# Delta rule: where the exponentials of the decays stand, and the yield inside the inverse

## The chip, the core and the metric

One core of one Trainium2 chip runs the whole program in one launch. The metric is the device time of that launch in microseconds (us). Of the kernel before there are three timed runs, and beside them one profiled execution, from which all rows below come.

## The reference

The reference is one layer for 4096 tokens of width 1024 in fp32. A modulated input `h` is projected by `w_in`. Half of the heads do gated linear attention (GLA), the other half the gated delta rule. Both results are gated with silu, projected back by `w_out`, and go through a residual and a layer norm. The part that matters here is the delta rule, with 4 heads of 128 and chunks of 64 tokens:

```
qkv = silu(causal_depthwise_conv(h @ w_qkv))      # q, k, v per head; q and k are l2-normed
d = cumsum(g)                                      # per chunk
L = exp(where(causal, d[:, None] - d[None, :], -inf))
A = where(strict, (beta * k) @ k.T * L, 0)
u, w = triangular_solve(A + eye, [beta * v, beta * k * exp(d)])
qk = where(causal, q @ k.T * L, 0)
for each chunk:                                    # scan over the chunks
    v_new = u - w @ S
    o = (q * exp(d)) @ S + qk @ v_new
    S = exp(d[-1]) * S + (k * exp(d[-1] - d)).T @ v_new
```

`L` is the matrix of decays. Its exponentials are the ones that the change moves.

## The kernel before, in words

The program has three stages one after the other: GLA (the span's start to about 730 us), the delta rule (730 to about 1860 us), and the output projection with the layer norm (to the end).

The delta-rule stage goes through 16 blocks: 2 pairs of heads, for each 8 blocks of 512 tokens. Iteration `it` of its loop overlaps three blocks: `new` is projected and prepared, `last` (the block before) is inverted and scanned, and `done` (two before) is normed. Each iteration has two halves. In each half `weave(side, main)` runs two generators against each other: `main` is a stream of projection matmuls (tile `pp`, 128x512, three per step and eight steps per projection), `side` is the small work. A `yield n` in `side` lets `main` go `n` steps on. Each matmul of `side` is bound behind the last `main` matmul emitted before it (`side_after`); once `main` has run out, that bound falls away.

In the first half `main` is `qk_products(new)`, 32 steps: four projections, each with a convolution (ACT `u` and `cacc`, then DVE `cacc`) and a Silu on ACT into `KQ`. `side` is `first_half`: `norm_gate(done)`, `new_values(last)`, a wait until two of the four projections are there, `decay_tiles(new)`, `inverse_head(last)`, `key_side(new)`, `inverse(last)`. In the second half `main` is `vg_products(new)`, and `side` is `second_half`: `gram(new)` and four steps of `scan(last)`.

- `decay_tiles` loads the tile `E` (128 x 8 x 128) by a DMA from `d_spill`, masks it on POOL (`affine_select`, L751), and makes eight Exp on ACT (rows `E<-E,dneg` at L104), with a load of the exp table ahead of them (L109).
- `key_side` transposes the keys (`pw<-ident,KQ`), squares them on ACT (eight rows `jk`, sums in `ssk`), and makes `kdec` on DVE.
- `inverse` forms the inverse of the lower-triangular block in three groups of small matmuls with a copy on ACT between them: group 1 is `pw<-Td,AQ` (32x32), copied to `Pa` (two ACT copies, L112); group 2 is `pw<-Rd,Pa` and `pw<-Pa,Rd` (32x32), copied to `TP` and `Rt`; then `pw<-TP,AQ` and `pw<-Rt,TP` (64x64), each with a copy. `Td` is a DVE transpose.
- `gram` (second half) multiplies `KQ` by itself (`pw<-KQ`, 128x256), and DVE makes `AQ` of it with `E` as a factor. It is the only reader of `E`.
- `scan` makes `pw<-S,KQ`, `zr` on DVE, `pw<-zr,Rt`, a copy `z` on ACT, `pw<-z,kdec`, and `S` on DVE. At its first step ACT still has rows `jk` (sums in `ssq`) of the queries.

The order of the instructions on each engine is not the order in which they are written: a scheduler with its own costs sets it. Two things bind it here: `side_after`, above, and `in_order`, by which all Exp, Ln and Silu and the table loads at L109 keep their written order. The load of the Silu table has no line of its own in the program. It appears at L104 ahead of the first Silu behind an Exp.

Matmuls of fp32 appear as two rows each in the trace, so the counts of small matmuls there are twice those of the program (rows that follow one another are merged, and some records can be missing).

Of the kernel before, what the change touches and what calls it, by code (L numbers as in the profile page):

```python
# [15 lines left out]
AF = mybir.ActivationFunctionType  # L16
# [14 lines left out]
def tile_hybrid(ctx, tc, xp, x, c, wada, bada, w_gla, w_vl, w_gdn, w_out, wup, bgate,  # L31
# [33 lines left out]
    def work_psum():  # L65
        return banks["work"].tile([P, TB], F32, name="pw", tag="pw")
# [15 lines left out]
    def in_order(ins):  # L82


        if last_table[0] is not None:
            keep_after(ins, last_table[0], "table order")
        last_table[0] = ins
# [9 lines left out]
    def mm(out, lhsT, rhs, start, stop):  # L97
        pe(nc.tensor.matmul(out, lhsT=lhsT, rhs=rhs, start=start, stop=stop))  # L98
# [4 lines left out]
    def act(out, in_, func, **kw):  # L103
        ins = nc.scalar.activation(out=out, in_=in_, func=func, **kw)  # L104
        if func in (AF.Exp, AF.Ln, AF.Silu):
            in_order(ins)

    def load_table():
        in_order(nc.scalar.preload_act_table_set("natural_log_exp_and_others"))  # L109

    def copy_a(out, in_):
        nc.scalar.copy(out=out, in_=in_)  # L112
# [158 lines left out]
    def gtile(name, dt=F32):  # L271
        return const.tile([P, 2, NC2], dt, name=name)

    beta, dmid, dneg, ed, edl, een = (gtile(n) for n in ("beta", "dmid", "dneg", "ed", "edl", "een"))
# [60 lines left out]
    with ExitStack() as ph:  # L335
# [300 lines left out]
        for it in range(2 * NB + 1):  # L636
            t, b = divmod(it, NB)
            new = it < 2 * NB
# [74 lines left out]
    with ExitStack() as ph:  # L713
# [29 lines left out]
        def decay_tiles(t, b, E):  # L743

            c0 = 8 * b
            nc.sync.dma_start(out=E.rearrange("p n c -> p (n c)"), in_=dsp[t, b:b + 1].to_broadcast([P, 8 * P]))
            load_table()
            for cc in range(2):
                ns = slice(4 * cc, 4 * cc + 4)
                Ec = E[:, ns, :]  # L750
                nc.gpsimd.affine_select(out=Ec, in_=Ec, compare_op=ALU.is_ge, fill=-1e30, base=0,  # L751
                                        pattern=[[0, 4], [1, P]], channel_multiplier=-1)
                for n in range(4 * cc, 4 * cc + 4):
                    act(E[:, n], E[:, n], AF.Exp, bias=dneg[:, t, c0 + n:c0 + n + 1])

        def sumsq(KQ, which, name):

# [14 lines left out]
        def key_side(st):  # L772

            t, c0, KQ = st["t"], 8 * st["b"], st["KQ"]
            ssk, kps = sumsq(KQ, 0, "ssk")
            f_ = dp2.tile([P, 8], F32, name="f_", tag="f_")
            nc.vector.reciprocal(out=f_, in_=ssk)
            tt(f_, f_, beta[:, t, c0:c0 + 8], mul)
            fe = dp2.tile([P, 8], F32, name="fe", tag="fe")
            tt(fe, f_, een[:, t, c0:c0 + 8], mul)  # L780
            kdec = dp2.tile([P, 8, P], F32, name="kdec", tag="kdec")
            for cc in range(2):
                tt(kdec[:, 4 * cc:4 * cc + 4, :], kps[cc].rearrange("p (n c) -> p n c", c=P),
                   fe[:, 4 * cc:4 * cc + 4].unsqueeze(2).to_broadcast([P, 4, P]), mul)
            yield 2

            s = power(dp2, ssk, half, "s")
            st.update(f_=f_, kdec=kdec, s=s)
# [46 lines left out]
        def inverse_head(st):  # L835

            Rd = st["Rd"]
            Td = dp.tile([P, 8, 32], F32, name="Td", tag="Td")
            nc.vector.transpose(out=Td.rearrange("p n i -> p (n i)"), in_=Rd.rearrange("p n i -> p (n i)"))
            for bl in range(4):  # L840
                bs = slice(32 * bl, 32 * bl + 32)
                nc.gpsimd.tensor_copy(out=Rt[bs, :, bs], in_=Rd[bs])
            for bl in range(2):
                bs = slice(32 * bl, 32 * bl + 32)
                copy_a(T64[bs, :, bs], Td[bs])
            st["Td"] = Td

        def inverse(st):

            AQ, Rd, Td = st["AQ"], st["Rd"], st["Td"]  # L850

            Pa = dp.tile([P, 8, 32], F32, name="Pa", tag="Pa")

            def bank():
                return work_psum().rearrange("p (n c) -> p n c", n=8)[:, :, 0:32]
            q = [slice(32 * i, 32 * i + 32) for i in range(4)]
            pp = [bank() for _ in range(2)]
            for j in range(8):
                for i in range(2):
                    top, bot = q[2 * i], q[2 * i + 1]  # L860
                    mm(pp[i][bot, j], lhsT=AQ[top, j, 0, bot], rhs=Td[top, j], start=True, stop=True)
            for i in range(2):
                copy_a(Pa[q[2 * i + 1]], pp[i][q[2 * i + 1]])
            yield 2
            pr, pt = [bank() for _ in range(2)], bank()
            for j in range(8):
                for i in range(2):
                    top, bot = q[2 * i], q[2 * i + 1]
                    mm(pr[i][top, j], lhsT=Pa[bot, j], rhs=Rd[bot, j], start=True, stop=True)
                mm(pt[q[1], j], lhsT=Rd[q[1], j], rhs=Pa[q[1], j], start=True, stop=True)  # L870
            act(T64[q[1], :, q[0]], pt[q[1]], AF.Copy, scale=-1.0)
            for i in range(2):
                act(Rt[q[2 * i], :, q[2 * i + 1]], pr[i][q[2 * i]], AF.Copy, scale=-1.0)
            yield 2

            pp = work_psum().rearrange("p (n c) -> p n c", n=8)
            for j in range(8):
                mm(pp[64:128, j], lhsT=AQ[0:64, j, 0, 64:128], rhs=T64[:, j], start=True, stop=True)
            copy_a(Pb[64:128], pp[64:128])
            yield 2  # L880
            pr = work_psum().rearrange("p (n c) -> p n c", n=8)
            for j in range(8):
                mm(pr[0:64, j], lhsT=Pb[64:128, j], rhs=Rt[64:128, j, 64:128], start=True, stop=True)
            act(Rt[0:64, :, 64:128], pr[0:64], AF.Copy, scale=-1.0)

        def new_values(st):
            vT, s = st["vT"], st["s"]
            vp = st["vp"] = dp.tile([P, 8, P], F32, name="vp", tag="vp")
            for cc in range(2):
                pv = work_psum()  # L890
                for j in range(4):
                    ch = 2 * cc + j // 2
                    transpose(pv[:, j * P:(j + 1) * P], in_=vT[j % 2][:, ch * P:(ch + 1) * P], identity=ident)
                tt(vp[:, 4 * cc:4 * cc + 4, :], pv.rearrange("p (n c) -> p n c", c=P),
                   s[:, 4 * cc:4 * cc + 4].unsqueeze(2).to_broadcast([P, 4, P]), mul)
                yield 1
# [43 lines left out]
        def norm_gate(st):  # L940

            o, ss, sg = st["vp"], st["ss"], st["sg"]
            stt(ss, ss, 1.0 / P, st["eq"], mul, add)
            r_ = power(dp2, ss, minus_half, "r_")
            tt(o, o, r_.unsqueeze(2).to_broadcast([P, 8, P]), mul)
            yield 10
            for hh in range(2):
                po = work_psum()
                for ch in range(4):
                    transpose(po[:, ch * P:(ch + 1) * P], in_=o[:, 2 * ch + hh], identity=ident)  # L950
                yield 1
                stt(sg[:, hh], po, dnw, sg[:, hh], mul, mul)
            nc.sync.dma_start(out=ysp[st["b"], 2 + st["t"]], in_=sg)
# [35 lines left out]
        def first_half(new, last, done):  # L989
            if done is not None:  # L990
                yield from norm_gate(done)
            if last is not None:
                yield from new_values(last)
            if new is not None:
                while new.get("there", 0) < 2:
                    yield 1
                decay_tiles(new["t"], new["b"], new["E"])
                if last is not None:
                    inverse_head(last)
                yield 8  # L1000
                yield from key_side(new)
            elif last is not None:
                inverse_head(last)
                yield 3
            if last is not None:

                yield 4 if done is not None else 10
                yield from inverse(last)

        def second_half(new, last):  # L1010
            if last is not None:
# [10 lines left out]
        for it in range(2 * NB + 2):  # L1022
            t, b = divmod(it, NB)
            new, last, done = None, sts.get(it - 1), sts.pop(it - 2, None)
            if it < 2 * NB:
                new = sts[it] = dict(t=t, b=b)
# [128 lines left out]
```

## Time and profile before

| | |
|---|---|
| runs (us) | 2149.45, 2152.29, 2164.0; median 2152.29 |
| profiled execution (us) | 2148.5, of it span 2146.8 |
| mean granted TensorE clock in the span | 0.988 |
| busy in the span | PE 2064.2, DVE 1320.7, ACT 956.6, POOL 228.1 |
| PE waits, 730 to 1860 us, for ACT `Pa` | 11.5 in 15 waits |

Busy shares are averages over three stages. PE is the matmul engine; PEld, the loading of its weights, runs beside it. A wait that a row shows in brackets is idle time of that engine ahead of the row, with what ended it. PEclk is the granted TensorE clock as a share of full speed: 1.00 is 2.4 GHz, 0.50 is 1.2 GHz.

### The profile page before, as it was taken

The numbers are of one execution on the slowest core, as the hardware profiler recorded it, in microseconds if no ns is written. First come the engines' busy times: TensorE is split into PE (matmuls) and PEld (weight loads), VectorE is DVE, ScalarE is ACT, GpSimd is POOL, SyncE is SP. The second block draws the span as 40 slices with busy tenths as digits, with TensorE's granted clock in tenths as the row PEclk, the third lists the DMA queues.
The fourth block names the chain that finished last, engine by engine and source line by source line (L and its number), as shares of the span: only waits on it lengthen the run. The fifth ranks groups of instructions, "written<-read, shape, count | busy, mean of one in ns | idle before, by whom it ended". The sixth has DMA issues, their size and how long they took to land.

```text
span 2146.8 us, 34571 instructions
## 1 busy us (share of the span) xinstructions
PE 2064.2 (96%) x12809; PEld 1743.0 (81%) x12809; DVE 1320.7 (62%) x3181; ACT 956.6 (45%) x2563; POOL 228.1 (11%) x430
## 2 busy tenths in 40 slices
PE   6899999999999999999999999999999999999998
PEld 5788888888888778887888878888888888788886
DVE  7785666445335676655666666665566666676665
ACT  2655555544454544554535665445544463121110
POOL 1000000000000221111210212101221110000000
PEclk9999999999999999998999999999999999999999
DMA  8575336423423544331332443333123354353321
GB/s 316 193 254 203 141 134 227 157 102 107 168 92 118 203 172 163 95 96 46 114 116 92 139 151 104 116 103 95 56 94 116 124 182 140 140 210 143 136 103 76
DMA packets 118585, 297.17 MB, mean 138 GB/s; under 512 B 45920, under 2 KB 48144, under 8 KB 117392
## 3 DMA queue, kind: packets, MB, share of 16 engines
q1 hardware_dynamic: 118416, 294.95, 40.1%
q8 instruction: 101, 1.65, 0.3%
q14 instruction: 68, 0.56, 0.1%
HBM read 213.84 MB, written 81.07 MB: 137 GB/s over the span
## 4 chain that ended last, share of the span: by engine, by line
PE 64%; DVE 11%; ACT 9%; DMA 8%; issue 3%; POOL 2%; SPq 2%; POOLq 0%; DVEq 0%; ACTq 0%
PE pp L98 48%; PE pw L98 15%; DMA lr_raw<-lr_spill 2%; ACT jk L104 2%; PE pw L101 2%; DMA xt<-xp 2%; ACT E L104 2%; DMA r_spill<-R 1%; DVE tp L69 1%; DVE R L69 1%; ACT L104 1%; DVE vp L69 1%; DMA Rd<-r_spill 1%; DVE cacc L72 1%; DVE W L69 1%
## 5 line engine op out<-in xcount | busy, mean ns | idle before, releaser
L98 PE MATMUL pp<-h,w 128*128 128x512 f32 x4512 | 1158.9, 402 | 1.2 <-DVE W L69 1.2
L98 PEld LDWEIGHTS pp<-h,w 128*128 128x128 f32 x4512 | 824.1, 189 | 157.8 <-issue 2.0
L98 PE MATMUL pp<-w,h 128*128 128x512 f32 (+1 forms) x2112 | 421.5, 355 | 11.8 <-ACT sg L104 10.6
L98 PEld LDWEIGHTS pp<-w,h 128*128 128x128 f32 x2112 | 349.1, 189 | 65.7 <-ACT sg L104 12.0
L72 DVE SCALAR_TENSOR_TENSOR cacc<-u,convw_sb,cacc 128x512 f32<-128x512 f32 x288 | 217.4, 756 | 127.0 <-ACT cacc L104 122.2
L98 PE MATMUL pp<-wvl,h 128*128 128x280 f32 x744 | 119.9, 310 | 34.9 <-ACT h L112 26.3
L98 PEld LDWEIGHTS pp<-wvl,h 128*128 128x128 f32 x744 | 105.6, 198 | 38.7 <-ACT h L112 29.4
L69 DVE TENSOR_TENSOR tp<-U,R 128x60 f32<-128x60 f32 (+24 forms) x496 | 104.3, 210 | 14.7 <-DMA U<-u_spill 3.0
L69 DVE TENSOR_TENSOR R<-R,tp 128x60 f32<-128x60 f32 (+24 forms) x496 | 104.2, 210 | 12.8
L498 DVE COPY VS<-pw 64x256 f32<-64x256 f32 x64 | 26.7, 417 | 135.5 <-PE pw L98 135.1
L112 ACT COPY u<-pp 128x512 f32<-128x512 f32 x96 | 55.9, 582 | 119.8 <-PE pp L98 109.9
L104 ACT ACTIVATE rl<-mv,lnepscol 128x1 f32<-128x1 f32 x32 | 9.4, 294 | 217.9 <-DVE mv L703 215.8
L261 POOL TENSOR_TENSOR rs<-ss,minus_half 128x8 f32<-128x8 f32 x16 | 31.4, 1962 | 606.7 <-DVE ss L514 606.7
L98 PE MATMUL pw<-S,KQ 128*128 128x128 f32 x512 | 84.4, 278 | 0.0
L98 PE MATMUL pw<-VS,W 128*128 128x128 f32 x512 | 81.3, 282 | 1.2 <-DVE VS L498 0.9
L104 ACT ACTIVATE jk<-pw 128x128 f32<-128x128 f32 x256 | 70.5, 276 | 26.5 <-PE pw L101 20.3
L72 DVE SCALAR_TENSOR_TENSOR S<-S,edl,pw 128x128 f32<-128x128 f32 x128 | 42.4, 344 | 61.6 <-PE pw L98 61.5
L98 PEld LDWEIGHTS pw<-S,KQ 128*128 128x128 f32 x512 | 74.0, 191 | 6.3 <-DVE S L72 2.4
L104 ACT ACTIVATE jk<-vp 128x128 f32<-128x128 f32 x128 | 39.9, 311 | 84.7 <-DVE vp L69 82.7
L72 DVE SCALAR_TENSOR_TENSOR xres<-xres,pp 128x512 f32<-128x512 f32 x48 | 32.4, 684 | 70.9 <-PE pp L98 66.7
L112 ACT COPY o<-pw 64x256 f32<-64x256 f32 x128 | 46.8, 366 | 63.7 <-DVE VS L502 33.8
L98 PEld LDWEIGHTS pw<-VS,W 128*128 128x128 f32 x512 | 70.6, 196 | 4.2 <-DVE VS L502 0.9
(287 smaller groups left out, 2759.0 us busy)
## 6 DMA issues: line engine op xcount, KB each, us to landing
h<-h_spill SPq DMA_DIRECT2D x192, 512.0 KB
h_spill<-h SPq DMA_DIRECT2D x64, 512.0 KB
xt<-xp SPq DMA_DIRECT2D x32, 512.0 KB
y_spill<-sg SPq DMA_DIRECT2D x32, 512.0 KB
yt<-y_spill SPq DMA_DIRECT2D x32, 512.0 KB
xres<-x SPq DMA_DIRECT2D x24, 512.0 KB
out_dram<-xres SPq DMA_DIRECT2D x24, 512.0 KB
mt<-wada SPq DMA_DIRECT2D x8, 1024.0 KB
```

The source lines that it names most:

```text
L69: nc.vector.tensor_tensor(out=out, in0=a, in1=b, op=op)
L72: nc.vector.scalar_tensor_tensor(out=out, in0=a, scalar=s, in1=b, op0=op0, op1=op1)
L98: pe(nc.tensor.matmul(out, lhsT=lhsT, rhs=rhs, start=start, stop=stop))
L101: pe(nc.tensor.transpose(out, in_=in_, identity=identity))
L104: ins = nc.scalar.activation(out=out, in_=in_, func=func, **kw)
L112: nc.scalar.copy(out=out, in_=in_)
L261: nc.gpsimd.tensor_tensor(out=y, in0=x, in1=e, op=ALU.pow)
L498: nc.vector.tensor_copy(out=VS[0:64, g, 1, :], in_=pm[0:64, 0:256])
```

## The change

`decay_tiles` keeps the DMA and the mask. Its table load and its eight Exp become a function `decay_exps`, which `first_half` calls as its last step, behind `inverse(last)`. Inside `inverse`, the yield between group 1 and group 2 is 3 instead of 2.

```diff
@@ -744,14 +744,17 @@
 
             c0 = 8 * b
             nc.sync.dma_start(out=E.rearrange("p n c -> p (n c)"), in_=dsp[t, b:b + 1].to_broadcast([P, 8 * P]))
-            load_table()
             for cc in range(2):
                 ns = slice(4 * cc, 4 * cc + 4)
                 Ec = E[:, ns, :]
                 nc.gpsimd.affine_select(out=Ec, in_=Ec, compare_op=ALU.is_ge, fill=-1e30, base=0,
                                         pattern=[[0, 4], [1, P]], channel_multiplier=-1)
-                for n in range(4 * cc, 4 * cc + 4):
-                    act(E[:, n], E[:, n], AF.Exp, bias=dneg[:, t, c0 + n:c0 + n + 1])
+
+        def decay_exps(t, b, E):
+            c0 = 8 * b
+            load_table()
+            for n in range(8):
+                act(E[:, n], E[:, n], AF.Exp, bias=dneg[:, t, c0 + n:c0 + n + 1])
 
         def sumsq(KQ, which, name):
 
@@ -861,7 +864,7 @@
                     mm(pp[i][bot, j], lhsT=AQ[top, j, 0, bot], rhs=Td[top, j], start=True, stop=True)
             for i in range(2):
                 copy_a(Pa[q[2 * i + 1]], pp[i][q[2 * i + 1]])
-            yield 2
+            yield 3
             pr, pt = [bank() for _ in range(2)], bank()
             for j in range(8):
                 for i in range(2):
@@ -1006,6 +1009,8 @@
 
                 yield 4 if done is not None else 10
                 yield from inverse(last)
+            if new is not None:
+                decay_exps(new["t"], new["b"], new["E"])
 
         def second_half(new, last):
             if last is not None:
```

The first place is PE around group 1 and group 2 of an inverse in a regular iteration (the tenth). `pp` are projection products, `pw` the small work. Before:

```order
L98 MATMUL pp<-h,w 128x512 x18
L98 MATMUL pw<-Td,AQ 32x32 x16
L98 MATMUL pp<-h,w 128x512 x11
L98 MATMUL pw<-Rd,Pa 32x32 x5
L98 MATMUL pw<-Pa,Rd 32x32
```

And now, in the same iteration:

```order
L98 MATMUL pp<-h,w 128x512 x18
L98 MATMUL pw<-Td,AQ 32x32 x16
L98 MATMUL pp<-h,w 128x512 x3
L98 MATMUL pw<-Rd,Pa 32x32 x2
L98 MATMUL pw<-Pa,Rd 32x32
```

Group 2 moves up from 11 products behind group 1 to 3. The other eight products come back further down, which is this piece of the difference, from the end of group 2 on:

```order
+L98 MATMUL pp<-h,w 128x512 x3
 L98 MATMUL pw<-TP,AQ 64x64 x8
 L98 MATMUL pp<-h,w 128x512 x4
 L98 MATMUL pw<-Rt,TP 64x64 x8
-L98 MATMUL pw<-KQ 128x256
-L98 MATMUL pp<-h,w 128x512 x2
-L98 MATMUL pw<-KQ 128x256 x3
+L98 MATMUL pp<-h,w 128x512 x8
+L98 MATMUL pw<-KQ 128x256 x2
+L98 MATMUL pp<-h,w 128x512 x3
+L98 MATMUL pw<-KQ 128x256 x2
```

Eight products now stand between the inverse's last group and the first matmul of `gram`.

The second place is ACT in a regular iteration. This is the difference down to the copies `Pa`:

```order
-L109 ACT_TABLE_LOAD
-L104 ACTIVATE E<-E,dneg 128x128 x8
 L112 COPY u<-pp 128x512
 L104 ACTIVATE cacc<-pp,convw_sb 128x512
 L104 ACTIVATE jk,ssk<-pw 128x128 x7
-L104 ACT_TABLE_LOAD
-L104 ACTIVATE KQ<-cacc 128x4x128
-L104 ACTIVATE jk,ssk<-pw 128x128
-L112 COPY Pa<-pw 32x256 x2
-L112 COPY u<-pp 128x512
```

Both table loads and the eight Exp are gone from ahead of `Pa`. They stand now at these places, later on the same engine:

```order
+L112 COPY TP<-pw 64x512
+L104 ACTIVATE KQ<-cacc 128x4x128
+L104 ACTIVATE Rt<-pw 64x8x64
+L109 ACT_TABLE_LOAD
+L104 ACTIVATE E<-E,dneg 128x128 x8
 L112 COPY u<-pp 128x512
 L104 ACTIVATE cacc<-pp,convw_sb 128x512
 L104 ACTIVATE jk,ssq<-pw 128x128 x6
+L104 ACT_TABLE_LOAD
 L104 ACTIVATE vT<-cacc 128x512
 L104 ACTIVATE jk,ssq<-pw 128x128 x2
```

The exp table is loaded behind the inverse's last copy, and the Silu table between the query squares of the second half.

The third place is DVE at the first scan step:

```order
-L72 SCALAR_TENSOR_TENSOR cacc<-u,convw_sb,cacc 128x512 x3
-L769 TENSOR_SCALAR ssq<-ssq 128x8
-L831 TENSOR_SCALAR ssq<-ssq 128x8
-L72 SCALAR_TENSOR_TENSOR zr<-pw,ed,vp 128x128 x2
+L72 SCALAR_TENSOR_TENSOR AQ<-pw,f__9680,E 128x256 x8
+L72 SCALAR_TENSOR_TENSOR cacc<-u,convw_sb,cacc 128x512 x3
+L72 SCALAR_TENSOR_TENSOR zr<-pw,ed,vp 128x128 x2
+L772 TENSOR_SCALAR ssq<-ssq 128x8
+L834 TENSOR_SCALAR ssq<-ssq 128x8
```

`zr` stood behind the two rows that read the squares' sums, and stands ahead of them now.

The first three inverses have an order of their own. There the changed kernel has 55, 53 and 24 products ahead of group 1, and in the first two the Exp stand ahead of the copies `TP<-Td` and `Pa`. On POOL and SP nothing of a regular iteration moves. The scheduler gives the changed kernel the same rows on all five queues whether the yield in `inverse` is 2 or 3, and so it does for the kernel before.

## Rows read from the trace of the kernel before

**Rows 1.** the page: busy us, share of the span and instructions by engine

```profile
PE 2064.2 (96%) x12809; PEld 1743.0 (81%) x12809; DVE 1320.7 (62%) x3181; ACT 956.6 (45%) x2563; POOL 228.1 (11%) x430
```

**Rows 2.** waits of PE, 730 to 1860 us: engine, line, releaser: us, times, longest

```profile
PE pw L98 <- ACT Pa L112: 11.5, 15, 1.6
PE pw L98 <- DVE Td L839: 2.1, 1, 2.1
...
PE pw L98 <- DVE ssk L769: 1.3, 1, 1.3
```

**Rows 3.** timeline of PE, one regular iteration: start, us, engine, line, operation, [idle before]

```profile
1397.10 0.69 PE L98 MATMUL pw<-Td,AQ 32*32 32x32 f32 x32
1397.72 2.79 PE L98 MATMUL pp<-h,w 128*128 128x512 f32 x11
1401.33 0.60 PE L98 MATMUL pw<-Rd,Pa 32*32 32x32 f32 x9 [0.83 <-ACT Pa L112]
...
1403.47 0.73 PE L98 MATMUL pw<-TP,AQ 64*64 64x64 f32 x9
```

**Rows 4.** timeline of ACT in the same iteration

```profile
1391.24 1.28 ACT L109 ACT_TABLE_LOAD   x1
1392.53 2.46 ACT L104 ACTIVATE E<-E,dneg 128x128 f32<-128x128 f32 x8
...
1398.71 1.28 ACT L104 ACT_TABLE_LOAD   x1
...
1400.92 0.75 ACT L112 COPY Pa<-pw 32x256 f32<-32x256 f32 x2
```

**Rows 5.** timeline of PE, the last inverse, which has no exponentials ahead

```profile
1795.97 0.69 PE L98 MATMUL pw<-Td,AQ 32*32 32x32 f32 x32
1796.59 0.96 PE L98 MATMUL pp<-w,h 128*128 128x512 f32 x3
1797.49 0.23 PE L98 MATMUL pw<-Rd,Pa 32*32 32x32 f32 x2
...
1799.25 1.14 PE L98 MATMUL pw<-TP,AQ 64*64 64x64 f32 x16
...
1801.45 0.73 PE L98 MATMUL pw<-Rt,TP 64*64 64x64 f32 x9
```

**Rows 6.** timeline of PE, three waits of over 1.5 us

```profile
863.11 0.84 PE L98 MATMUL pw<-Td,AQ 32*32 32x32 f32 x32 [2.08 <-DVE Td L839]
...
999.14 0.60 PE L98 MATMUL pw<-Rd,Pa 32*32 32x32 f32 x9 [1.64 <-ACT Pa L112]
...
1665.41 0.60 PE L98 MATMUL pw<-Rd,Pa 32*32 32x32 f32 x9 [1.61 <-ACT Pa L112]
```

**Rows 7.** windows: us, busy time by engine (x), PEclk, DMA share, GB/s

```profile
863.60:866.90 3.30, 3.30 (x20) 2.66 (x15) 0.76 (x5) 3.16 (x9) 0.57 (x1) 0.50 0.00 0
1000.00:1013.60 13.60, 13.60 (x72) 10.51 (x63) 4.77 (x9) 3.49 (x8) 0.95 (x3) 0.50 0.00 1
1664.00:1670.00 6.00, 4.59 (x76) 3.51 (x77) 4.17 (x9) 4.56 (x12) 1.96 (x3) 1.00 0.01 3
1795.90:1803.00 7.10, 7.10 (x129) 5.49 (x128) 3.87 (x4) 4.45 (x12) 0.00 (x0) 1.00 0.02 6
```

**Rows 8.** timeline of DVE in the regular iteration

```profile
1401.78 1.29 DVE L69 TENSOR_TENSOR kdec<-pw,fe 128x512 f32<-128x512 f32 x2
...
1408.81 1.66 DVE L72 SCALAR_TENSOR_TENSOR AQ<-pw,f__14235,E 128x256 f32<-128x256 f32 x4 [3.50 <-PE pw L98]
```

**Rows 9.** timeline of ACT at its first scan step

```profile
1416.73 0.28 ACT L104 ACTIVATE jk<-pw 128x128 f32<-128x128 f32 x1
...
1418.96 0.37 ACT L112 COPY z<-pw 128x256 f32<-128x256 f32 x1 [1.86 <-PE pw L98]
```

**Rows 10.** timeline of PE at its first scan step

```profile
1419.90 0.61 PE L98 MATMUL pw<-z,kdec 128*128 128x128 f32 x4
```

## The prediction, made before the changed kernel ran

> **What bounds the kernel now.** I read the page first, then the waits of PE in the delta-rule stage, then the timelines of PE and ACT around one inverse, and last the granted clock behind the longest waits. On the page PE is busy 96% of the span, ACT 45% [rows 1]: time is to be had where PE stands still, or where it runs at half clock. The waits of PE in this stage are nearly one thing: 11.5 us in 15 waits for ACT's copy `Pa` [rows 2]. Two single ones, 2.1 us for `Td` and 1.3 us for `ssk`, are in the first two inverses. In a regular iteration group 1 starts at 1397.10, 11 products follow, and group 2 still waits 0.83 us for `Pa` [rows 3]. ACT says why: the exp table (1.28 us), eight Exp (2.46 us) and the Silu table (1.28 us) stand ahead of `Pa`, which starts only at 1400.92 [rows 4], while group 1 had ended at 1397.79. The last inverse has no Exp ahead; there group 2 starts 1.52 us behind group 1's start, with three products between them and no wait [rows 5].
>
> The waits have a second price. Behind the wait of 2.08 us at 863 and that of 1.64 us at 999 [rows 6] the granted clock was 0.50, that is 1.2 GHz, for 3.3 and for 13.6 us with PE busy throughout; behind the wait of 1.61 us at 1665 it stayed at 1.00 [rows 7].
>
> **The change, part by part.** *The three steps.* No cost and no gain: group 1 comes at step 31 of 32, so that a yield of 2 or of 3 both exhaust the products, and the order of no queue depends on it. All that follows comes from the Exp.
>
> *The waits for `Pa`.* Without the 1.28 + 2.46 + 1.28 = 5.02 us of ACT, `Pa` could start at 1400.92 - 5.02 = 1395.90, before group 1 has ended. So group 1's end releases it, as in the last inverse, and the new order with three products there is the last inverse's order. The 11.5 us go. Group 2 and its four products also take 1403.47 - 1401.33 = 2.14 us to `TP` behind a wait, and 1799.25 - 1797.49 = 1.76 us without one [rows 3, 5]. That would be 0.38 us more in each of 13 iterations, 4.9 us at most and none at least. I take a third, 1.7 us, since the two iterations run different products in between and the new order has three, not four.
>
> *The first two inverses.* They have 55 and 53 products ahead of group 1 now, so I let the waits of 1.3 and 2.1 us go. But here the Exp stand ahead of `Pa`. Where they did so before, the mean wait was 11.5 / 15 = 0.77 us: two of these cost 1.5. Net gain 1.9 us. The ends: 3.4 us if nothing waits, and 3.4 - 2 x (1.28 + 2.46) = -4.1 us if nothing covers a load and the Exp.
>
> *The clock.* The two stretches lost (3.3 + 13.6) / 2 = 8.5 us. With the waits ahead of them gone I let them go too; the other end is 0.
>
> *The work that is moved.* One exp table, eight Exp and one Silu table in each iteration, now in and behind the inverse's end; DMA and mask of `E` stay. ACT has room, so the cost is nothing while two covers hold. First, `AQ` needs `E`. By the last inverse, the final group starts 5.48 us behind group 1 and is done about 1.1 us later [rows 5]; its copy ends near 7.2, the table near 8.5, and the first Exp near 8.8, with the others every 2.46 / 8 = 0.31 us. The eight products (0.3 us each, [rows 5]) and the first pair of `gram` bring the first `AQ` to about 9.3, and each `AQ` takes 1.66 / 4 = 0.42 us [rows 8]. So `E` is half a microsecond ahead and stays ahead; without that cover `AQ` and the bank that it frees come late by as much as `E` does. Second, the Silu table now stands among the query squares. ACT has 1.86 us idle ahead of `z` [rows 9], the table takes 1.28: 0.58 us are left, and `z`, done at 1419.33, has 0.57 us more before PE uses it at 1419.90 [rows 10]. `zr`, which stood behind the squares' sums, now stands ahead of them, so it isn't held.
>
> **A rule that speaks against it.** In the trace a switch of tables costs its row: the first Exp starts 1.29 us after its load does [rows 4]. The Trainium skill, "ScalarE: Activation LUTs", section "What ACT_TABLE_LOAD costs", gives about 1283 ns for the load and about 1380 ns of drain, 2.66 us for each switch. The row agrees with the load; no run shows the drain, and by that rule the sum would end some 12 us later, as in the fourth rival below.
>
> **The sum.** 11.5 + 1.7 + 1.9 + 8.5 = 23.6 us off the profiled execution's 2148.5, which makes 2124.9. The median of the runs, 2152.29, stands 3.8 above that execution; I carry half of it, 1.9 us, and predict **2127 us**. One per cent, about what a measurement of this kernel tells from no change, is 21.5 us: faster begins below 2130.8, slower above 2173.8.
>
> **The rivals.**
>
> *The forecast* (0.45): 2127, with its own range 2118 to 2132, from the refill at its full 4.9 us to a new wait of about 0.4 us in each of 13 iterations.
>
> *The waits go, the clock's loss stays* (0.20). For it: granted half clock is tied to two places only, and a new pause in the first inverses can begin another stretch. Against it: the wait of 1.61 us left it alone [rows 6, 7], and I expect shorter ones. 2127 + 8.5 = 2135.
>
> *The wait takes another name* (0.18). Group 2 comes some 2.7 us earlier than before, and one of its banks is read by `kdec` on DVE, which takes 1.29 us [rows 8] and hangs on the same ACT squares. If half of the mean wait returns, 13 x 0.4 = 5.2, with the clock's loss: 2141. With the first inverses at their bad end (6.0 us worse than taken) it is 2147.
>
> *A table switch holds ACT longer than its row* (0.08), as long again, 1.28 us. The first Exp then comes at 10.1 instead of 8.8, 0.8 us behind the first `AQ`; `z` is 2 x 1.28 - 1.86 = 0.70 late, 0.13 beyond its cover. 13 x (0.8 + 0.13) = 12: 2139. Against it: the 1.29 us of rows 4.
>
> *Slower: the clock falls in most iterations* (0.09). The inverse is packed now: group 2, `TP` and `Rt` come within 7 us with 10 products among them instead of 19. Both half-clock stretches of this stage begin among such small matmuls [rows 6, 7]. If each of 13 iterations took a stretch of 13.6 us, that is 13 x 6.8 = 88 us on 2135: 2223; stretches of 3.3 us give 21 us, 2156. It is slower by over 1% from six long stretches on (6 x 6.8 = 41, 2176). Against it: the last inverse has this packing, and its clock was 1.00 [rows 7].
>
> That the change doesn't do what it says is true of its second half, and priced: the three steps do nothing.
>
> **Range and chances.** 2117 to 2147 leaves out the last rival and little else. Faster by over 1%: 0.45 (the forecast nearly whole, and the best ends of the second). Within 1%: 0.48 (all others up to a few long stretches). Slower: 0.07 (the upper part of the last).
>
> **What would show it.** In the profile of the changed kernel the waits of PE for `Pa` should be a few tenths in all past the third inverse, group 2 should start about 1.5 us behind group 1, and the first `pw<-ident,KQ` of the second half should come about a microsecond earlier behind `Td`. `E` should end before the third `AQ`, ACT should still idle ahead of the first `z`, and PEclk should be 1.00 from 863 to 1020. The sum is wrong if PE waits for `kdec`, `TP` or `AQ` instead, if new waits of over 1.6 us stand in the first two inverses, or if half clock appears in the regular iterations.

## The result, and the profile after

The changed kernel takes 2128.96 us in the median of three runs (2128.13 to 2138.52), before it was 2152.29. The ratio is 0.9886, with a 95% interval of 0.9855 to 0.9917: faster by 1.1%. The interval leaves out 1; the one per cent that the prediction takes as its bound lies inside it. The profiled execution takes 2128.13 us, with a span of 2126.4, against a span of 2146.8 before: 20.4 us less.

The waits of PE in the delta-rule stage come first, in the columns of [rows 2]:

```profile
PE pw L98 <- DVE Td L842: 3.1, 3, 1.3
PE pw L101 <- ACT KQ L104: 2.5, 5, 0.8
...
PE pw L98 <- ACT TP L104: 1.8, 10, 0.2
...
PE pw L98 <- ACT Pa L112: 0.5, 1, 0.5
```

The 11.5 us for `Pa` are 0.5, and that half is in the first inverse. Small waits came instead: `TP`, 0.17 to 0.19 us in ten inverses, and three for `Td` where one had been: 1.3 us each in the second and the third inverse and 0.5 in the eighth. The timeline of PE for the tenth inverse, the one of [rows 3]:

```profile
1383.02 0.69 PE L98 MATMUL pw<-Td,AQ 32*32 32x32 f32 x32
1383.64 0.96 PE L98 MATMUL pp<-h,w 128*128 128x512 f32 x3
1384.53 0.23 PE L98 MATMUL pw<-Rd,Pa 32*32 32x32 f32 x2
...
1386.32 1.14 PE L98 MATMUL pw<-TP,AQ 64*64 64x64 f32 x16 [0.19 <-ACT TP L104]
...
1391.54 1.02 PE L98 MATMUL pw<-KQ 128*128 128x256 f32 x4
...
1393.09 1.02 PE L98 MATMUL pw<-KQ 128*128 128x256 f32 x4
```

Group 2 starts 1.51 us behind group 1's start (4.23 before, [rows 3]), as in the last inverse [rows 5]. ACT in the same iteration, against [rows 4]:

```profile
1383.74 0.75 ACT L112 COPY Pa<-pw 32x256 f32<-32x256 f32 x2 [1.60 <-PE pw L98]
...
1389.70 0.59 ACT L104 ACTIVATE Rt<-pw 64x512 f32<-64x512 f32 x1 [0.74 <-PE pw L98]
1390.31 1.28 ACT L109 ACT_TABLE_LOAD   x1
1391.60 2.45 ACT L104 ACTIVATE E<-E,dneg 128x128 f32<-128x128 f32 x8
...
1403.87 0.37 ACT L112 COPY z<-pw 128x256 f32<-128x256 f32 x1 [0.43 <-PE pw L98]
```

Now ACT waits 1.60 us for PE ahead of `Pa`, where PE waited for ACT before. The Silu table among the query squares leaves 0.43 us ahead of `z`. DVE at `gram`, against [rows 8]:

```profile
1392.67 0.88 DVE L72 SCALAR_TENSOR_TENSOR AQ<-pw,f__14226,E 128x256 f32<-128x256 f32 x2 [4.37 <-ACT E L104]
1394.22 0.88 DVE L72 SCALAR_TENSOR_TENSOR AQ<-pw,f__14226,E 128x256 f32<-128x256 f32 x2 [0.68 <-PE pw L98]
...
1397.34 0.88 DVE L72 SCALAR_TENSOR_TENSOR AQ<-pw,f__14226,E 128x256 f32<-128x256 f32 x2 [0.68 <-PE pw L98]
```

The row names `E` as what ended the first wait, but the times say otherwise. PE's first pair of `gram` ends at 1392.56 and its second at 1394.11, and both times `AQ` starts 0.11 us behind. The first of the eight Exp alone ends at 1392.00, 0.67 us ahead of the first `AQ`. So PE releases both, and `E` is half a microsecond early, as the prediction has it. The granted clock over the stretch that had the two half-clock pieces of [rows 7]:

```profile
863.00:1020.00 157.00, 153.52 (x1078) 127.27 (x1077) 95.11 (x278) 83.82 (x247) 28.31 (x64) 1.00 0.29 89
```

PEclk is 1.00 throughout. Where the 20.4 us lie can be read from one kind of row that stands at the same place of the work in both kernels, the first `pw<-ident,vT` of a block. Before, in the third block and in the last:

```profile
913.28 0.60 PE L101 MATMUL pw<-ident,vT 128*128 128x128 f32 x4
...
1779.34 1.04 PE L101 MATMUL pw<-ident,vT 128*128 128x128 f32 x8
```

And after:

```profile
910.72 0.60 PE L101 MATMUL pw<-ident,vT 128*128 128x128 f32 x4
...
1758.98 1.03 PE L101 MATMUL pw<-ident,vT 128*128 128x128 f32 x8
```

Between the two rows 866.06 us became 848.26: 17.8 us less, 6.8 of them the clock's stretch behind 999, so 11.0 for the rest. The listed waits of PE between the two rows fell by only 6.5 us, from 13.5 to 7.0: the 11.5 for `Pa` went, and 5.0 of others came (`TP` 1.8, `Td` 1.8, `KQ` 1.1, the rest 0.3). The other 4.5 us stand in no listed wait: PE took less time for the same work. The prediction calls this the refill, the time that the same matmuls take longer behind a wait. Ahead of the first row 2.56 us were gained: GLA ended 1.05 us later (its last `pw<-ident,o` at 727.89 instead of 726.84; nothing of the change lies there, and three executions of the changed kernel's rows put that end up to 3.2 us apart), the first blocks took 3.6 us less, 1.7 of them the clock's stretch behind 863. Behind the last row nothing changed (367.5 and 367.4 us).

### The profile page after: what moved, and what is told of

Read it like the earlier page. It is cut to its first block, busy times and chain, and to the rows that moved or that the text cites. A ratio compares the mean times of both kernels' runs of the same rounds, so it can differ in the third digit from the quotient of the medians.

```text
span 2126.4 us, 34605 instructions
## 1 busy us (share of the span) xinstructions
PE 2052.1 (97%) x12809; PEld 1732.7 (81%) x12809; DVE 1327.4 (62%) x3181; ACT 959.2 (45%) x2563; POOL 231.2 (11%) x430
## 4 chain that ended last, share of the span: by engine, by line
PE 74%; DVE 9%; DMA 7%; ACT 5%; issue 2%; POOL 1%; SPq 1%; POOLq 0%; DVEq 0%; ACTq 0%
PE pp L98 57%; PE pw L98 15%; PE pw L101 3%; DMA lr_raw<-lr_spill 2%; DMA xt<-xp 2%; DVE R L69 1%; DVE tp L69 1%; DVE cacc L72 1%; DVE vp L69 1%; DMA r_spill<-R 1%; DMA mt<-wada 1%; DVE W L69 1%; DVE h L69 1%; DMA wt<-wada 1%; ACT jk L104 1%
## 5 line engine op out<-in xcount | busy, mean ns | idle before, releaser
L104 ACT ACTIVATE jk<-pw 128x128 f32<-128x128 f32 x256 | 70.8, 277 | 26.4 <-PE pw L101 20.4
L104 ACT ACTIVATE KQ<-cacc 128x512 f32<-128x512 f32 x64 | 40.3, 630 | 83.0 <-DVE cacc L72 82.6
```

## The experiments

### Which half of the change acts

```diff
 # Exp moved, the yield put back (exps_only)
-            yield 3
+            yield 2
             pr, pt = [bank() for _ in range(2)], bank()
```

> The changed kernel with the yield inside the inverse put back to 2: the Exp alone are moved. The rows of all five queues are those of the changed kernel. Theory (all comes from the Exp): 2127 to 2131 in undisturbed runs. Rival (the three steps do half or more): 2138 or above.

Measured: 2130.03 us (2128.89 to 2133.27), ratio to before 0.9888 [0.9856, 0.9919].

```diff
 # the kernel before, with the yield alone (yield3_only)
-            yield 2
+            yield 3
             pr, pt = [bank() for _ in range(2)], bank()
```

> The kernel before with the yield of 3 alone, Exp in their old place. The rows of all five queues are those of the kernel before. Theory: no difference, ratio 1.00 within half a per cent, 2148 to 2154. Rival (the three steps do half or more): 2140 or below. It also says how far two builds of the same rows differ.

Measured: 2154.53 us, ratio 0.9992 [0.9966, 1.0018]. The three steps do nothing, with the Exp in either place. The whole effect is the Exp's. Single runs of these same rows lie between 2138.51 and 2160.48, which says how far one run of the kernel before can be trusted.

### Is it the wait, or PE's new order?

The change did two things to PE at once: `Pa` comes earlier, and the scheduler packed the inverse. One kernel has the packed order with the Exp in their old place, one the loose order with the Exp late.

```diff
 # compact_early: the kernel before, second-half products bound behind group 2
     def pe(ins):
+        last_pe[0] = ins
+        if behind[0] is not None:
+            keep_after(ins, behind[0], "group 2 first")
...
+            group2[0] = last_pe[0]
             act(T64[q[1], :, q[0]], pt[q[1]], AF.Copy, scale=-1.0)
...
+                    behind[0] = group2[0]
                     proj_k(ps, ws[i], h, k)
+                    behind[0] = None
```

> The kernel before, Exp in their old place, but the products of the second half are bound behind group 2, so that PE has the changed kernel's packed order (three products between group 1 and group 2). Theory (the gain is the wait for Pa that goes; the order is only what the scheduler makes of it; clock falls behind long waits): Pa is still ready only about 4.2 us behind group 1's start, so each of some 13 inverses waits about 2.7 us instead of 0.8: 13 x 1.9 = 25 us slower than before, about 2174, and since these waits are longer than 1.64 us, half clock follows many of them, 1.7 to 6.8 us each: 2185 to 2250. Rival A (the packed order itself is the gain): as the changed kernel, 2129 to 2140. Rival B (half clock has nothing to do with the waits): about 2174, with no more half clock than before.

Measured: 2240.91 us (2238.31 to 2246.94), ratio 1.0396 [1.0357, 1.0435]. The same inverse on PE:

```profile
1381.75 0.69 PE L102 MATMUL pw<-Td,AQ 32*32 32x32 f32 x32
1382.37 0.96 PE L102 MATMUL pp<-h,w 128*128 128x512 f32 x3
1386.76 0.64 PE L102 MATMUL pw<-Rd,Pa 32*32 32x32 f32 x9 [3.43 <-ACT Pa L116]
...
1388.14 2.07 PE L102 MATMUL pp<-h,w 128*128 128x512 f32 x4
```

And its windows (us, busy times, PEclk, DMA share, GB/s):

```profile
1387.00:1399.50 12.50, 12.50 (x96) 9.77 (x94) 3.62 (x6) 4.08 (x9) 1.58 (x3) 0.50 0.00 1
1399.50:1405.00 5.50, 5.50 (x26) 4.67 (x24) 2.63 (x6) 0.56 (x2) 0.00 (x0) 0.96 0.00 0
```

PE waits 3.43 us and then runs 12.5 us at half clock; four products take 2.07 us instead of 1.19. In this stage the waits for `Pa` are 36.2 us (11.5 before), and the clock's loss (each 2 us window times 1 - PEclk) is 87.0 us (8.5 before); one wait of 8.1 us for `ssk` in the first inverse comes on top. These are shares and no sum: they add up to more than the 98.4 us by which the spans differ, since some half clock falls into the waits themselves. Packing without an early `Pa` makes the kernel 4% slower. Of the cost the smaller part is the waits, the larger the clock behind them. The theory holds; rivals A and B fall.

```diff
 # loose_late: the changed kernel, group 1 four steps earlier, group 2 four behind it
-                yield 4 if done is not None else 10
+                if done is None:
+                    yield 10
                 yield from inverse(last)
...
-            yield 3
+            yield 4
             pr, pt = [bank() for _ in range(2)], bank()
```

> The changed kernel with the Exp late, but group 1 four steps earlier and group 2 four steps behind it, so that 12 products stand between them as in the kernel before (11). Theory (only the wait counts): no wait for Pa, within 3 us of the changed kernel, 2126 to 2132. Rival A (packing saves work of its own, the 0.38 us an iteration of the prediction's refill, or more): 5 to 13 us slower than the changed kernel, 2134 to 2142.

Measured: 2125.23 us (2122.12 to 2129.09), ratio 0.9864 [0.9831, 0.9897]. With 12 products between the groups the kernel is as fast as with 3, if not a little faster. So packing gains nothing by itself, and rival A is out. (A small difference the other way is taken up with the last runs.)

### Does the clock follow the length of the wait?

```diff
 # wait_dose: the changed kernel, packed order forced as above, Pa copied more often
+MORE = {3: 3, 4: 6, 5: 4, 6: 8, 7: 2, 8: 5, 9: 7, 10: 4, 11: 6, 12: 3, 13: 5, 14: 8}
...
             for i in range(2):
-                copy_a(Pa[q[2 * i + 1]], pp[i][q[2 * i + 1]])
+                for _ in range(1 + (0 if i else MORE.get(8 * st["t"] + st["b"], 0))):
+                    in_order(copy_a(Pa[q[2 * i + 1]], pp[i][q[2 * i + 1]]))
```

> The changed kernel with PE's packed order forced, and in the inverses of blocks 3 to 14 the first copy Pa made 2 to 8 times more (3, 6, 4, 8, 2, 5, 7, 4, 6, 3, 5, 8; 61 copies of about 0.36 us in all), so that each inverse waits by a dose of its own; the copies write the same values. Theory: each wait is the dose, some 0.7 to 4 us with u and cacc now and then in between, 22 to 35 us in all, and half clock follows the waits above about 1.6 us and not the shorter ones: 6 to 9 stretches, 10 to 60 us lost. In all 2160 to 2220. Rival (half clock comes at random, or by the block): as many stretches behind short waits as behind long ones, or none.

Measured in one run: 2233.32 us, above the 2160 to 2220 expected. The waits for `Pa` are 39.0 us in all, 2.22 to 5.25 us in the twelve dosed inverses, longer than I expected, so that the dose has no short end. Half clock followed every one of them. The two dosed inverses with waits of 2.22 us had it too, and the inverses of the two blocks without a dose ahead of them, with 0.19 us, had none. (The first inverse, without a dose too, waited 8.6 us for `Td` and had half clock.) So half clock is not random; nor is it a matter of the block, since the same blocks had none in the changed kernel. To have short waits as well I counted all profiles of this study together: every wait of PE of 0.6 us or more in this stage, and whether PEclk fell below 0.90 within the next six us:

| wait of PE | followed by half clock | lost each time, us |
|---|---|---|
| 1.7 us or more | 30 of 30 | 1.7 to 7.2 |
| 1.4 to 1.7 us | 6 of 8 | 1.7 to 6.8 |
| 1.0 to 1.4 us | 4 of 30 | 5.1 to 6.8 |
| 0.6 to 1.0 us | 5 of 37 | 5.1 to 6.8 |

The lost time is the sum of 1 - PEclk over windows of 1 us behind the wait. Where two waits lie close together one stretch is counted for both. The classes were drawn when the waits were known, and 28 of the 30 in the first row come from the two kernels that were made to wait, compact_early and wait_dose. The other way round the count is as clear: all 40 stretches of half clock in this stage begin inside a wait of 0.8 us or more, or at most 2.7 us behind one.

### How late may the exponentials come?

```diff
 # exps_later: the changed kernel, the inverse's last copy six times
-            act(Rt[0:64, :, 64:128], pr[0:64], AF.Copy, scale=-1.0)
+            for _ in range(6):
+                act(Rt[0:64, :, 64:128], pr[0:64], AF.Copy, scale=-1.0)
```

> The changed kernel with the inverse's last copy Rt made six times instead of once, so that table and Exp come up to 3 us later on ACT (same values; PE's order in the delta-rule stage is unchanged). By the prediction's cover (E is half a microsecond ahead of AQ, and PE pays what E is late beyond that): AQ is 1 to 2.5 us late and 12 x 0.5 to 2 us = 6 to 24 us are lost: 2135 to 2153. Rival, from the trace of the changed kernel, where the first AQ already waits for E and PE doesn't: AQ catches up between the pairs of gram (0.88 us of each 1.55), so that PE loses nothing: 2127 to 2132.

Measured: 2128.18 us (2122.41 to 2133.51), ratio 0.9888 [0.9844, 0.9932]. Nothing is lost. (That the first `AQ` waits for `E`, as the rival has it, does not hold, as shown at its rows; here the first Exp ends at 1393.51, 0.19 us ahead of the first `AQ`.) But the test was weak: the scheduler put the Exp between the copies, the first `AQ` came no later (2.98 us behind the start of `Rt`, 2.97 in the changed kernel), and only the last Exp were over 2 us late. So I made all of them late:

```diff
 # exps_twice: the changed kernel, eight Exp into a scratch tile ahead
             load_table()
+            for n in range(8):
+                jk = dp.tile([P, P], F32, name="jk", tag="jk")
+                act(jk, E[:, n], AF.Exp, bias=dneg[:, t, c0 + n:c0 + n + 1])
             for n in range(8):
                 act(E[:, n], E[:, n], AF.Exp, bias=dneg[:, t, c0 + n:c0 + n + 1])
```

> The changed kernel with eight more Exp (of the same tiles, written to a scratch tile) between the exp table and the eight that count, so that all of E comes 2.5 us later; PE's order in a regular iteration is unchanged. In the run with the repeated Rt the first two pairs of AQ hardly came later, since the Exp that they need stood between the copies; here they do. By the prediction's cover: AQ starts 2.5 us later and PE pays about 2 us in each of 13 iterations, 26 us: about 2155. Rival (AQ takes 0.88 us of the 1.55 us between two pairs of gram, four banks hold the pairs, and the next matmuls that want one come 6 us behind the first pair): AQ starts 2.5 us later, has caught up by half of that at its last pair, and PE loses nothing or the few tenths by which zr or the Silu table come late: 2128 to 2136.

Measured: 2129.07 us (2123.9 to 2131.36), ratio 0.9903 [0.9867, 0.9939]. ACT, DVE and PE in the tenth inverse, which starts at 1387.10:

```profile
1395.68 3.44 ACT L104 ACTIVATE jk<-E,dneg 128x128 f32<-128x128 f32 x8
1399.03 2.43 ACT L104 ACTIVATE E<-E,dneg 128x128 f32<-128x128 f32 x8
```

```profile
1399.44 3.23 DVE L72 SCALAR_TENSOR_TENSOR AQ<-pw,f__14386,E 128x256 f32<-128x256 f32 x8 [7.07 <-ACT E L104]
```

```profile
1401.86 1.03 PE L101 MATMUL pw<-ident,KQ 128*128 128x128 f32 x8
```

Behind group 1 `E` is 3.35 us later than in the changed kernel, and `AQ` starts at 12.34 us instead of 9.65, 2.69 later: what is missing is the 0.67 us that `E` was ahead. Now `E` does hold `AQ`, which starts 0.03 us behind the end of the first Exp. It then runs all eight in one piece, where it had waited for PE between the pairs. The first `pw<-ident,KQ` comes 14.76 us behind group 1, as in the changed kernel (1397.78 - 1383.02 = 14.76). PE pays nothing.

### A version that beats both

In the third and the eighth inverse of the changed kernel PE waits for `Td` (1.3 and 0.5 us), because DVE makes the transpose behind the key squares' sum and `kdec`. I bound it ahead from the fourth iteration on, in the changed kernel and in the loose one.

```diff
 # after_td, loose_td
-            nc.vector.transpose(out=Td.rearrange("p n i -> p (n i)"), in_=Rd.rearrange("p n i -> p (n i)"))
+            td_last[0] = nc.vector.transpose(out=Td.rearrange("p n i -> p (n i)"), in_=Rd.rearrange("p n i -> p (n i)"))
...
-            nc.vector.tensor_scalar_add(out=acc, in0=acc, scalar1=RMS_EPS)
+            ins = nc.vector.tensor_scalar_add(out=acc, in0=acc, scalar1=RMS_EPS)
+            if which == 0 and td_first[0]:
+                keep_after(ins, td_last[0], "Td first")
```

> The changed kernel once more, as the yardstick of this comparison. 2127 to 2132.

> The loose order with late Exp once more, beside the changed kernel. If the 2125.2 against 2130.0 of the run before was real (it lacks ten waits for TP of 0.17 to 0.19 us, 1.8 us in all), it comes out 2 to 5 us below the changed kernel again. If it was a matter of which execution had a half-clock stretch, within 2 us.

> The loose order with late Exp, and on DVE the transpose Td bound ahead of the key squares' sum from the fourth iteration on, so that PE's wait for Td in the third inverse (1.3 us) and in the eighth (0.5 us) goes. By the rows alone 1.8 us below the loose order; where the wait of 1.3 to 1.6 us in the third inverse was followed by half clock, 5 to 7 us more in that execution, so that the slowest runs come down too. About 2121 to 2126. Rival (other waits take their place): as the loose order.

> The changed kernel with only the transpose Td bound ahead as in the run beside it. 1.8 us below the changed kernel by the rows, more where half clock followed the wait: 2123 to 2129.

Measured, side by side on one chip:

| | median, us | runs, us | ratio to before |
|---|---|---|---|
| changed kernel again | 2130.8 | 2128.09 to 2132.76 | 0.9896 [0.9869, 0.9922] |
| loose order again | 2128.72 | 2128.27 to 2136.01 | 0.9894 [0.9866, 0.9921] |
| loose order, `Td` first | 2125.62 | 2118.49 to 2129.7 | 0.9867 [0.9838, 0.9896] |
| changed kernel, `Td` first | 2124.78 | 2119.02 to 2127.24 | 0.9866 [0.9838, 0.9894] |

The loose order's median is 2.1 us below the packed one's, at the border between its two forecasts, and the runs overlap: the runs don't tell the two apart, and the 5 us of the run before did not come again. The rows do show a small gain: four regular iterations, from one block's first `pw<-ident,vT` to the next one's, take 258.97 us in the changed kernel (1303.45 to 1562.42) and 258.00 in loose_late (1304.13 to 1562.13), 0.24 us less each, most of it the wait for `TP`. `Td` first is better: every run of it in the changed kernel lies below every run of the changed kernel itself, by 6.0 us in the medians; in the loose order the runs overlap, and the medians are 3.1 us apart. The rows promise 1.8; in three of the other executions (the Exp alone, the Exp later, the loose order again) the same wait of 1.44 to 1.60 us was followed by 5.1 to 6.8 us lost to half clock. With `Td` first that wait is gone from the waits of PE behind 900:

```profile
PE pw L98 <- ACT TP L104: 1.8, 10, 0.2
PE pw L101 <- DVE vp L69: 1.8, 3, 1.2
...
PE pw L101 <- ACT KQ L104: 0.8, 1, 0.8
PE pw L98 <- DVE ssk L772: 0.4, 1, 0.4
```

Does half clock make up the other 4 us? Each timed run lists the granted clock of its span. Its mean is 0.9918 in the five runs of the changed kernel and 0.9924 in the five with `Td` first; 0.0006 of 2125 us is 1.3 us (an estimate). In the loose order it is 0.9892 and 0.9920, by the same working 6 us, where the mean times differ by 5.5. So the clock can be the gain in the loose order, but not the most of it in the changed kernel, where some 3 us stay open.

## Why the prediction was right, and where not

The forecast was 2127, the time 2128.96. The forecast sum took 23.6 us off the profiled execution; the spans give 20.4. The mechanism was right; that the total came so near is partly luck, since terms that were off cancelled.

*The three steps.* Forecast nothing; 0.9992 and the pair 0.9888 and 0.9886 show it.

*The waits for `Pa`.* Forecast 11.5 + 1.7 = 13.2 us, measured 11.0 from the third block on. The mechanism is as told: group 1's end releases `Pa`, group 2 starts 1.51 us behind (1.52 forecast), and the wait is 0. But two terms were off, one each way. The refill was put at a third of its 4.9 us, 1.7, and came out at about 4.5. In the tenth iteration this can be read from the first `pw<-ident,KQ` of the second half, before and after:

```profile
1412.86 1.03 PE L101 MATMUL pw<-ident,KQ 128*128 128x128 f32 x8
```

```profile
1397.78 1.04 PE L101 MATMUL pw<-ident,KQ 128*128 128x128 f32 x8
```

Behind the start of group 1 that is 15.76 and 14.76 us. Of the 1.00 us the waits are 0.83 - 0.19 = 0.64, so 0.36 are refill, close to the 0.38 that the prediction read. And new waits, put at nothing, cost 5.0 us. The one for `TP` comes with the packed order, for the loose one has none; those for `Td` don't, for loose_late and loose_again have 2.4 and 2.9 us of them. The prediction named a wait for `TP` as a sign of being wrong: so the rival that the wait takes another name came true to that part, by `TP`, `Td` and `KQ` and not by `kdec`.

*The first two inverses.* Forecast 1.9; the first blocks took 3.6 us less, of which the clock's 1.7, so 1.9. The number is right and the way only in part: in the first inverse the wait for `ssk` (1.32) gave way to 0.49 for `Pa`, as forecast, but in the second `Td` did not go (2.08 became 1.29) and no wait for `Pa` came. A wait of 1.20 us for `KQ` at 749.75 went too, which the sum did not have.

*The clock.* Forecast 8.5; both stretches are gone in the profiled execution. A single execution says little here: the same rows as the changed kernel's, profiled again twice, had one stretch each (6.8 us behind a wait of 1.60 us at 925, and 5.1 us behind waits of 0.64 and 1.05 us at 870), and the rows of the kernel before, profiled again in yield3_only, lost 15.4 us instead of 8.5. The granted clock that each timed run lists gives the mean: on one chip 0.9868 in 13 runs of the kernel before and 0.9900 in the four of exps_only, on another 0.9874 in 11 and 0.9918 in the five of the changed kernel again. As shares of some 2140 us that is 7 and 9 us, an estimate over the whole span. It bears the 8.5 out, and speaks against the rival that the waits go and the clock's loss stays, though in one execution or another a part of it stays.

*The packing rival.* That the packed inverse lowers the clock by itself is excluded: PEclk is 1.00 over 13 packed inverses, and the packed order with a late `Pa` has half clock behind each long wait. Long waits do it.

*The moved work.* Forecast: no cost, and right. The first cover is as told: the first Exp ends 0.67 us ahead of the first `AQ` (half a microsecond forecast), and the last ends at 1394.05, ahead of the third `AQ` at 1394.22. That `AQ` comes late once `E` is later than that is right too, by exps_twice. What was wrong is the next step, in the fourth rival: that a late `AQ` is paid by PE, 0.8 us in each iteration. In exps_twice `AQ` is 2.69 us later and PE pays nothing, since `AQ` needs 3.23 us in one piece and had 5.55 us (1392.67 to 1398.22). For PE the cover is the space between the pairs of `gram`, not `E`'s lead. The Silu table left 0.43 us ahead of `z` (0.58 forecast).

*The table's price.* By the Trainium skill, "ScalarE: Activation LUTs", section "What ACT_TABLE_LOAD costs", a drain of about 1380 ns stands beside the load's 1283. After the change too the first Exp starts 1.29 us behind its load, and the `Rt` ahead of that load ends at 1389.70 + 0.59 = 1390.29, 0.02 us ahead of it. The load agrees; no drain shows, and the measurement decides. Had it been there, exps_twice shows that the part on `E` would have cost nothing either: the price of 10 us that this rival carried for it (13 x 0.8) was no price for PE.

*From profile to median.* I carried 1.9 us; the median stands 0.8 above the profiled execution. That is 1.1 us less than carried, and GLA's 1.05 us, which no term had, happen to make up for it.

## What to carry to other kernels

Price a wait of a busy TensorE not by its length alone: in this stage every wait of 1.7 us or more was followed by half clock, and that cost 1.7 to 7.2 us more, at most some three times the wait itself. When an engine is ahead of the critical one's next need, ask what else stands in its queue before that need, and move what is needed later behind it; look for the reader's slack (here `AQ`'s gaps), not for the producer's lead. Check what a row names as the end of a wait against the times: here it named `E`, and PE's matmuls had ended the wait. And where a scheduler sets the order, compare the orders before costing an edit: half of this edit moved no instruction.

## What the runs showed of the hardware that was not expected

The granted clock falls behind waits of PE, and the longer the wait, the surer: 30 of 30 waits of 1.7 us or more were followed by 1.2 GHz, 9 of 67 between 0.6 and 1.4 us, and six of these nine stand within 3 us of another wait (a like pair in exps_only was not followed by it). In between the length alone does not decide: in the one profile of yield3_only waits of 1.60 us were followed by 1.2 GHz at 863 and at 999 and not at 1668. The length of what follows doesn't grow with the wait: behind 5.25 us 6.4 us were lost, behind 2.22 us between 3.4 and 6.8. A table load takes 1.28 us and lets the next activation start 1.29 to 1.30 us behind its start, with no further pause on either side.
